# Larger row blocks in fewer places: a masked prefix sum read from HBM in blocks of 1024 rows

**Chip, cores, metric.** One core of one Trainium2 chip. The metric is the device time of one execution in microseconds (us), the median of several executions. An execution over 1.5% above the fastest of the same kernel is called slow. A verdict is "same", "faster" or "slower" against a bound of 2%, and "unclear" where the interval lies across it.

**Words.** The engines are TensorE (matrix products, PE in the profiles), VectorE (DVE), ScalarE (ACT), GpSimd (POOL) and SyncE (SP, which issues most loads). A *descriptor* is one contiguous piece of a transfer, one packet in the transfer records (of 2 to 16 KB for the rows of x); the page shows 16 transfer engines. The *granted clock* is TensorE's clock as a share of full speed: in the kernel before, eight matmuls of a block took 1.90 us where it was 0.5 (at 44.47 us), sixteen of the rests the same 1.90 us where it was 1.0 (at 72.95). The *landing records* are the trace's 16 marks per transfer, one for each engine's part; a transfer has landed with the last of them. All times in a trace count from the span's start. A timeline line reads: start, duration, engine, line, operation, what it writes <- what it reads, shapes, count, and in brackets the idle time before it and what ended it.

## The reference

```python
B, S, D = 8, 8192, 512          # x: [B, S, D] float32, w: [D, D], lengths: [B]
mask = (pos < lengths[:, None, None])
cs = np.cumsum(x * mask, axis=1)
mid_features = cs[b_idx, lengths // 2, :]
return np.matmul(mid_features[:, None, :], w).squeeze(1)
```

Row `lengths // 2` of the prefix sum is the sum of the first n = min(lengths // 2 + 1, lengths) rows of each batch. So the kernel reads n rows per batch (14,680 of 65,536 in this draw), adds them with matmuls, and multiplies the eight sums by `w`. With 2 KB per row it is a kernel that reads.

## The kernel before

Rows come in three kinds. **Blocks** have 512 rows and go through seven places in turn; the first blocks of batches 0 and 1 are loaded *blind*, before the lengths are known. What is left of a batch is its **rest**, up to 511 rows, loaded in parts of 256, 128, 64 and at most 64 rows into one of two rest places, which are zeroed once. One more block of the last batch (**`last`**) is loaded at the very end and folded in after the sum. The recorded texts call the blocks *items*, counted from 0, and rest 0 to rest 7 are those of batches 0 to 7; the loop takes one place after another in rounds, and each of the first four rounds adds two rests.

```python
    G = 4
    BLK = P * G                 # 512 rows, 8 KB per partition and descriptor
    BLIND = 2
    NS = 7
    PARTS = [(256, 0, 2, 4), (128, 1, 4, 4), (64, 3, 4, 2)]
    # ... (cut)
    def take(eng, s, n):                       # wait for n and take it back
        eng.wait_ge(s, n).then_inc(s, -n)

        def load(k):                           # SyncE: refill place k when it is free
            take(sp, s_free[k], 1)
            sp.dma_start(
                out=xt[:, k], in_=xf[ds(sp.snap(at[k]), BLK)].rearrange("(p g) d -> p g d", g=G)
            ).then_inc(s_full[k], 16)
    # ... (cut: ScalarE loads the rests, VectorE works out weights and addresses)
        with pe.Fori(0, pe.snap(rounds, min_val=B // 2, max_val=ROUNDS)):   # TensorE
            def add_item(k):
                keep_busy()                    # two bf16 matmuls on nothing, for the clock
                take(pe, s_full[k], 16)
                for j in range(G):
                    mm = add(j, cur[:, k], xt[:, k, j])
                mm.then_inc(s_done[k], 1)      # VectorE then sets new weights and frees the place
            nested(pe, left, BLIND, add_item)
            with pe.If_cmp(rest_rounds, 1, "IS_GE"):
                for q in range(2):
                    take(pe, s_rem[q], 16 * (len(PARTS) + 1))
                    for j in range(G):
                        mm = add(j, cur_rem[:, q, j * B:(j + 1) * B], rem[:, q, j])
                    mm.then_inc(s_rdone[q], 1)
            nested(pe, left, NS, add_item, BLIND)
        tell()                                 # the signal: the sum is complete
    # ... (cut: copy, fold with last, transpose, product with w, output)
```

## Time and profile before

| | before |
|---|---|
| median of the first 3 executions | 86.8 us (86.62 to 87.42) |
| span of the profiled execution | 84.9 us |
| read from HBM | 31.23 MB, 419 GB/s between 10 and 76.5 us |
| TensorE matmul busy | 56.6 us (67% of the span) |
| VectorE, ScalarE, GpSimd busy | 18.7, 3.7, 3.0 us |

### The profile page before, as it was taken

The numbers are of one execution on the slowest core, as the hardware profiler recorded it, in microseconds if no ns is written. First come the engines' busy times: TensorE is split into PE (matmuls) and PEld (weight loads), VectorE is DVE, ScalarE is ACT, GpSimd is POOL, SyncE is SP. The second block draws the span as 40 slices with busy tenths as digits, with TensorE's granted clock in tenths as the row PEclk, the third lists the DMA queues.
The fourth block names the chain that finished last, engine by engine and source line by source line (L and its number), as shares of the span: only waits on it lengthen the run. The fifth ranks groups of instructions, "written<-read, shape, count | busy, mean of one in ns | idle before, by whom it ended". The sixth has DMA issues, their size and how long they took to land. (4 is left out here: it accounts for less than half of the span.)

```text
span 84.9 us, 1511 instructions
## 1 busy us (share of the span) xinstructions
PE 56.6 (67%) x387; PEld 10.8 (13%) x391; DVE 18.7 (22%) x94; ACT 3.7 (4%) x5; POOL 3.0 (4%) x11
## 2 busy tenths in 40 slices
PE   2602000699999999984609855998528699999730
PEld 2002000101111112111000101211101011212410
DVE  3788888600200101100000000101000000002320
ACT  3910000000000000000000000000000000000020
POOL 5061000000000000000000000000000000000000
PEclk9999999999999999999995799999997556999999
DMA  2899999999999999999999999999999999993000
GB/s 39 309 417 428 404 422 420 422 413 424 428 428 428 413 409 428 413 413 424 428 394 424 424 428 413 413 428 424 424 403 430 424 421 409 422 403 129 2 1 14
DMA packets 4839, 31.30 MB, mean 369 GB/s; under 512 B 674, under 2 KB 690, under 8 KB 1218
## 3 DMA queue, kind: packets, MB, share of 16 engines
q1 hardware_dynamic: 3906, 27.27, 77.4%
q10 hardware_dynamic: 928, 3.97, 12.0%
q8 instruction: 2, 0.03, 0.1%
q14 instruction: 3, 0.02, 0.1%
HBM read 31.23 MB, written 0.02 MB: 368 GB/s over the span
## 5 line engine op out<-in xcount | busy, mean ns | idle before, releaser
L449 PE MATMUL s_ps<-xt,cur 128*8 128x512 f32 x200 | 30.2, 679 | 10.4 <-PEq L138 10.4
L462 PE MATMUL idle_ps<-idle 128*128 128x512 bf16 x46 | 16.4, 436 | 8.9 <-DVE addr L290 8.3
L413 DVE TENSOR_TENSOR cur<-since 128x8 f32 x18 | 3.1, 173 | 34.7 <-DVEq L138 34.7
L449 PE MATMUL s_ps<-rem,cur_rem 128*8 128x512 f32 x64 | 7.6, 592 | 0.0
L462 PEld LDWEIGHTS idle_ps<-idle 128*128 128x128 bf16 x50 | 2.9, 100 | 32.5 <-issue 32.5
L449 PEld LDWEIGHTS s_ps<-xt,cur 128*8 128x8 f32 x200 | 3.3, 87 | 23.6 <-issue 23.6
L290 DVE COPY s_sb<-s_ps 128x256 f32<-128x256 f32 x2 | 0.9, 426 | 18.7 <-PE idle_ps L466 18.7
L263 ACT COPY o_sb<-o_ps 8x128 f32<-8x128 f32 x2 | 0.5, 258 | 76.8 <-PE o_ps L529 76.8
L473 PE MATMUL s_ps<-zero 1*128 1x512 f32 x2 | 2.1, 1135 | 1.5 <-DVE zero L290 1.5
L476 PE MATMUL n_ps<-n_f,ones 1*128 1x8 f32 x2 | 0.6, 368 | 3.3 <-DVE n_f L290 3.3
L449 PEld LDWEIGHTS s_ps<-rem,cur_rem 128*8 128x8 f32 x64 | 1.8, 93 | 5.5 <-issue 5.5
L422 DVE COPY cur_rem<-table 128x32 f32 x6 | 1.1, 182 | 3.8 <-DVEq L138 3.8
L215 ACT ACTIVATE rem<-rem 128x2048 uint32<-128x2048 uint32 x1 | 1.9, 1909 | 0.0
L279 POOL MEMSET rem<- 128x2048 f32 x1 | 1.8, 1804 | 2.9 <-DVE addr L290 2.9
L290 DVE CAST n_f<-n_i 1x8 f32<-1x8 int32 x1 | 1.7, 1656 | 0.0
L529 PE MATMUL o_ps<-wt,t_sb 128*8 128x128 f32 x32 | 1.1, 273 | 0.5 <-DVE t_sb L290 0.5
L215 ACT ACT_TABLE_LOAD x1 | 1.3, 1283 | 1.3 <-PEq L552 1.3
L455 PE MATMUL t_ps<-last,e_last 128*8 128x128 f32 x32 | 1.2, 273 | 0.1
L476 PEld LDWEIGHTS n_ps<-n_f,ones 1*128 1x128 f32 x2 | 0.5, 308 | 4.8 <-DVE n_f L290 4.8
L290 DVE TENSOR_TENSOR part_a<-since,step_a 1x35 f32<-1x35 f32 (+1 forms) x2 | 1.0, 518 | 0.1
L529 PEld LDWEIGHTS o_ps<-wt,t_sb 128*8 128x8 f32 x32 | 0.8, 89 | 0.7 <-issue 0.7
L290 DVE TENSOR_TENSOR since<-item,begin 1x35 f32<-1x35 int32 (+1 forms) x2 | 0.8, 401 | 0.1
(68 smaller groups left out, 14.2 us busy)
## 6 DMA issues: line engine op xcount, KB each, us to landing
xt<-in_x_dram SPq DMA_DIRECT2D x25, 1024.0 KB, 16.3
rem<-in_x_dram ACTq DMA_DIRECT2D x3, 512.0 KB, 6.9
wt<-in_w_dram ACTq DMA_DIRECT2D x1, 1024.0 KB, 7.4
last<-in_x_dram SPq DMA_DIRECT2D x2, 512.0 KB, 17.4
rem<-in_x_dram ACTq DMA_DIRECT2D x3, 256.0 KB, 6.3
rem<-in_x_dram ACTq DMA_DIRECT2D x3, 128.0 KB, 6.5
rem<-in_x_dram ACTq DMA_DIRECT2D x3, 32.0 KB, 5.8
rem<-in_x_dram ACTq DMA_DIRECT2D x1, 64.0 KB, 6.0
```

Source lines behind the costliest of these rows:

```text
L215: act.memzero(rem[:, 0]).then_inc(s_rfree[0], 1)
L263: copy = act.copy(out=o_sb[1][:, j * P:(j + 1) * P], in_=o_ps[64 + 32 * j:64 + 32 * j + B, :P])
L279: pool.memset(rem[:, 1], 0.0).then_inc(s_rfree[1], 1)
L290: do(*args, **kw).then_inc(s_dve, 1)
L413: dve.tensor_tensor(out=cur[:, k], in0=since[:, :B, here].rearrange("p b o -> p (b o)"), in1=since[:, 1:, here].rearrange("p b o -> p (b o ...
L422: dve.tensor_copy(out=cur_rem[:, q], in_=rests[:, ds(dve.snap(of, min_val=1, max_val=B // 2 - 1), 1), q].rearrange("p o w -> p (o w)"),).t ...
L449: return pe.matmul(s_ps[32 * j:32 * j + B], lhsT=weights, rhs=rows, start=False, stop=False, skip_group_check=True, tile_position=(0, 32 * j))
L455: return pe.matmul(t_ps[32 * j:32 * j + B, :P], lhsT=weights, rhs=row[:, P * j:P * (j + 1)], start=False, stop=False, skip_group_check=Tru ...
L462: pe.matmul(idle_ps[:], lhsT=idle[:, :P], rhs=idle[:], start=True, stop=True)
L473: pe.matmul(s_ps[:], lhsT=zero[:], rhs=zero[:, :1].to_broadcast((1, D)), start=True, stop=False, skip_group_check=True)
L476: pe.matmul(n_ps[:, :B], lhsT=ones[:], rhs=n_f[:], start=True, stop=True).then_inc(s_pe, 1)
L529: mm = pe.matmul(o_ps[32 * j:32 * j + B, :P], lhsT=t_sb[:, kc, :B], rhs=wt[:, kc, j * P:(j + 1) * P], start=(kc == 0), stop=(kc == KC - 1) ...
```

## The change

The intent: fewer, larger transfers. Blocks become 1024 rows (16 KB per partition), three places in place of seven. The two blind loads become half blocks that share place 0; `last` is a half block too. Rests grow to up to 1023 rows, in five parts. Both rest places are zeroed by ScalarE; four idle matmuls in place of two run ahead of each block, which is meant to keep the clock up. In each round the first rest is added behind the second block, the second rest behind the third. The core of the diff:

```diff
-    G = 4
+    G = 8
     BLK = P * G
-    BLIND = 2
-    NS = 7
+    HALF = BLK // 2
+    FROM, TO = 2, B - 1
+    NS = 3
-    PARTS = [(256, 0, 2, 4), (128, 1, 4, 4), (64, 3, 4, 2)]
+    PARTS = [(512, 0, 2, 0, 8), (256, 1, 4, 0, 8), (128, 3, 4, 0, 4), (64, 3, 4, 4, 6)]
@@ blind loads
-            out=xt[:, b], in_=xf[b * S:b * S + BLK].rearrange("(p g) d -> p g d", g=G)
-        ).then_inc(s_full[b], 16)
+            out=xt[:, 0, b * (G // 2):(b + 1) * (G // 2)],
+            in_=xf[b * S:b * S + HALF].rearrange("(p g) d -> p g d", g=G // 2),
+        ).then_inc([s_blind, s_full[0]][b], 16)
@@ ScalarE
-        act.memzero(rem[:, 0]).then_inc(s_rfree[0], 1)
-        act.wait_ge(s_len1, 16)
+        for q in range(2):
+            act.memzero(rem[:, q]).then_inc(s_rfree[q], 1)
+        act.wait_ge(s_dve, DVE_LEFT)
@@ GpSimd
-        pool.memset(rem[:, 1], 0.0).then_inc(s_rfree[1], 1)
@@ TensorE
-            for _ in range(2):
+            for _ in range(4):
                 pe.matmul(idle_ps[:], lhsT=idle[:, :P], rhs=idle[:], start=True, stop=True)
@@ TensorE's round (VectorE's follows it)
-            nested(pe, left, BLIND, add_item)
-            (rest 0, rest 1)
-            nested(pe, left, NS, add_item, BLIND)
+            nested(pe, left, NS - 1, add_item)
+            add_rest(0)
+            nested(pe, left, NS, add_item, NS - 1)
+            add_rest(1)
```

More of the change, by code (lines that the diff above doesn't have):

```diff
@@ L46 @@
     B, S, D = x.shape
-    G = 4
+    G = 8
     BLK = P * G
-    BLIND = 2
-    NS = 7
-    ROUNDS = -(-(B * S // 2 // BLK - 1) // NS)
+    HALF = BLK // 2
+    FROM, TO = 2, B - 1
+    NS = 3
+    ROUNDS = -(-(B * S // 2 // BLK + 1) // NS)
     ITEMS = ROUNDS * NS
     KC = D // P
-    PARTS = [(256, 0, 2, 4), (128, 1, 4, 4), (64, 3, 4, 2)]
+    PARTS = [(512, 0, 2, 0, 8), (256, 1, 4, 0, 8), (128, 3, 4, 0, 4), (64, 3, 4, 4, 6)]
     WT = G * B
@@ L76 @@
     xt = sb("xt", [P, NS, G, D])
-    last = sb("last", [P, G, D])
+    last = sb("last", [P, G // 2, D])
     rem = sb("rem", [P, 2, G, D])
@@ L81 @@
     n_i = sb("n_i", [1, B], I32)
-    n_f = sb("n_f", [1, B])
+    n_f = sb("n_f", [1, 2, B])
     ones = sb("ones", [1, P])
@@ L85 @@
     idle = sb("idle", [P, D], BF16)
-    special = sb("special", [P, B])
+    special = sb("special", [1, B])
+    half1 = sb("half1", [1, B])
+    left2 = sb("left2", [1, B, 2], I32)
+    first_i = sb("first_i", [1, B], I32)
     one8 = sb("one8", [P, B])
-    cnt, blocks, has, usual, begin = [sb(n, [P, B + (n == "begin")], I32 if n in ("cnt", "blocks") else F32)
-                                      for n in ("cnt", "blocks", "has", "usual", "begin")]
-    blocks1, has1, usual1, begin1 = [sb(n + "1", [1, B + (n == "begin")], I32 if n == "blocks" else F32)
-                                     for n in ("blocks", "has", "usual", "begin")]
+    cnt, has, blocks, usual, begin = [sb(n, [P, B + (n == "begin")], I32 if n in ("cnt", "blocks") else F32)
+                                      for n in ("cnt", "has", "blocks", "usual", "begin")]
+    blocks1, usual1, begin1 = [sb(n + "1", [1, B + (n == "begin")], I32 if n == "blocks" else F32)
+                               for n in ("blocks", "usual", "begin")]
     step_c = sb("step_c", [1, B - 1])
@@ L105 @@
     meta = sb("meta", [1, 4], I32)
-    cur = sb("cur", [P, NS, B])
+    cur = sb("cur", [P, 2, NS, B])
     e_last = sb("e_last", [P, B])
@@ L132 @@
     s_last = [sem(f"last{h}") for h in range(2)]
-    s_w, s_len1, s_out = sem("w"), sem("len1"), sem("out")
+    s_w, s_len1, s_blind, s_out = sem("w"), sem("len1"), sem("blind"), sem("out")
     s_pool, s_dve, s_pe, s_act = sem("pool"), sem("dve"), sem("pe"), sem("act")
@@ L149, in less @@
         eng.reg_alu(n, n, 0, ALU.max)
-    DVE_SEL, DVE_ADDR, DVE_N, DVE_MASK, DVE_ALL = 2, 21, 23, 56, 64
+    DVE_SEL, DVE_ADDR, DVE_LEFT, DVE_N, DVE_MASK, DVE_ALL = 2, 22, 24, 26, 62, 70
     DVE_LAST = DVE_ALL + 6
@@ L159 @@
     nc.scalar.dma_start(out=wt[:], in_=w.rearrange("(p kc) d -> p kc d", kc=KC)).then_inc(s_w, 16)
-    for b in range(BLIND):
+    for b in range(FROM):
         nc.sync.dma_start(
-            out=xt[:, b], in_=xf[b * S:b * S + BLK].rearrange("(p g) d -> p g d", g=G)
-        ).then_inc(s_full[b], 16)
+            out=xt[:, 0, b * (G // 2):(b + 1) * (G // 2)],
+            in_=xf[b * S:b * S + HALF].rearrange("(p g) d -> p g d", g=G // 2),
+        ).then_inc([s_blind, s_full[0]][b], 16)
     block = nc.Block(no_gpsimd_drain=True)
@@ L185, in _ @@
         sp.wait_ge(s_dve, DVE_ADDR)
-        sp.load([left] + at[BLIND:], addr[:, BLIND - 1:NS])
-        nested(sp, left, NS, load, BLIND)
+        sp.load([left] + at[1:], addr[:, :NS])
+        nested(sp, left, NS, load, 1)
         sp.wait_ge(s_dve, DVE_ALL)
@@ L198, in _ @@
         with sp.If_cmp(facts[2], 1, "IS_GE"):
-            from_rows = xf[ds(sp.snap(facts[3]), BLK)].rearrange("(p g) d -> p g d", g=G)
+            from_rows = xf[ds(sp.snap(facts[3]), HALF)].rearrange("(p g) d -> p g d", g=G // 2)
             for h in range(2):
@@ L209, in _ @@
         alu = act.reg_alu
-        base, at, t = [act.alloc_register(f"act_{n}") for n in ("base", "at", "t")]
+        at, t = [act.alloc_register(f"act_{n}") for n in ("at", "t")]
         words = [act.alloc_register(f"act_n{i}") for i in range(4)]
         pair, top = act.alloc_register("act_pair"), 2 * B - 4
-        act.reg_mov(base, 0)
         act.reg_mov(pair, 0)
-        act.memzero(rem[:, 0]).then_inc(s_rfree[0], 1)
-        act.wait_ge(s_len1, 16)
+        for q in range(2):
+            act.memzero(rem[:, q]).then_inc(s_rfree[q], 1)
+        act.wait_ge(s_dve, DVE_LEFT)
         with act.Fori(0, B // 2):
-            act.load(words, lens1[:, ds(act.snap(pair, min_val=0, max_val=top), 4)])
+            act.load(words, left2[:].rearrange("o b n -> o (b n)")[:, ds(act.snap(pair, min_val=0, max_val=top), 4)])
             for q in range(2):
-                n = words[2 * q]
-                alu(t, n, 1, ALU.logical_shift_right)
-                alu(t, t, 1, ALU.add)
-                alu(n, t, n, ALU.min)
+                n, base = words[2 * q:2 * q + 2]
                 take(act, s_rfree[q], 1)
-                for count, start, step, g in PARTS:
+                for count, start, step, a, b in PARTS:
                     alu(t, n, count, ALU.bitwise_and)
@@ L230, in _ @@
                         act.dma_start(
-                            out=rem[start::step, q, :g],
-                            in_=rows(act, at, base, t, count).rearrange("(p g) d -> p g d", g=g),
+                            out=rem[start::step, q, a:b],
+                            in_=rows(act, at, base, t, count).rearrange("(p g) d -> p g d", g=b - a),
                         ).then_inc(s_rem[q], 16)
@@ L240, in load_last @@
                 def load_last(count):
-                    to = rem[3::4, q, 2:] if count > 32 else rem[3:4 * count:4, q, 2:3]
+                    to = rem[3::4, q, 6:] if count > 32 else rem[3:4 * count:4, q, 6:7]
                     act.dma_start(
@@ L256, in _ @@
                             act.sem_inc(s_rem[q], 16)
-                alu(base, base, S, ALU.add)
             alu(pair, pair, 4, ALU.add)
@@ L270, in _ @@
         pool.iota(item[:], pattern=[[1, ITEMS]], base=0, channel_multiplier=0)
-        pool.iota(item_a[:], pattern=[[BLK, ITEMS]], base=BLK - BLIND * BLK, channel_multiplier=0)
+        pool.iota(item_a[:], pattern=[[BLK, ITEMS]], base=HALF - BLK, channel_multiplier=0)
+        pool.iota(first_i[:], pattern=[[S, B]], base=0, channel_multiplier=0)
         pool.iota(pid[:], pattern=[[0, 1]], base=0, channel_multiplier=1)
@@ L274, in _ @@
         pool.iota(fold_i[:], pattern=[[-1, B]], base=128, channel_multiplier=1).then_inc(s_pool, 1)
-        for k in range(BLIND, NS):
+        for k in range(1, NS):
             pool.sem_inc(s_free[k], 1)
         pool.memset(idle[:], 1.0).then_inc(s_pool, 1)
-        pool.wait_ge(s_dve, DVE_ADDR)
-        pool.memset(rem[:, 1], 0.0).then_inc(s_rfree[1], 1)
     @block.vector
@@ L299, in _ @@
         step(dve.memset, special[:], 0.0)
-        step(dve.memset, special[:, :BLIND], 1.0)
-        step(dve.memset, special[:, B - 1:], 1.0)
+        step(dve.memset, special[:, :FROM], float(HALF))
+        step(dve.memset, special[:, TO:], float(HALF))
         step(dve.memset, one8[:], 1.0)
         step(dve.memset, step_c[:], float(S))
-        step(dve.memset, step_c[:, BLIND - 1:BLIND], float(S - BLK))
+        step(dve.memset, step_c[:, FROM - 1:FROM], float(S - HALF))
         dve.wait_ge(s_len1, 16)
@@ L309, in _, with begins @@
         step(dve.tensor_tensor, out=n_i[:], in0=n_i[:], in1=lens1[:, ::2], op=ALU.min)
-        def begins(cnt, blocks, has, usual, begin):
+        step(dve.scalar_tensor_tensor, out=half1[:], in0=n_i[:], scalar=float(HALF), in1=special[:],
+             op0=ALU.is_ge, op1=ALU.mult)
+        step(dve.tensor_tensor, out=left2[:, :, 0], in0=n_i[:], in1=half1[:], op=ALU.subtract)
+        def begins(cnt, blocks, usual, begin):
             parts = blocks.shape[0]
-            step(dve.tensor_scalar, out=blocks[:], in0=cnt[:], scalar1=9, scalar2=None,
+            step(dve.tensor_scalar, out=blocks[:], in0=cnt, scalar1=10, scalar2=None,
                  op0=ALU.logical_shift_right)
-            step(dve.scalar_tensor_tensor, out=has[:], in0=blocks[:], scalar=1.0, in1=special[:parts],
-                 op0=ALU.is_ge, op1=ALU.mult)
-            step(dve.tensor_tensor, out=usual[:], in0=blocks[:], in1=has[:], op=ALU.subtract)
+            step(dve.tensor_copy, out=usual[:], in_=blocks[:])
             step(dve.tensor_tensor_scan, out=begin[:, 1:], data0=one8[:parts], data1=usual[:],
-                 initial=float(BLIND), op0=ALU.mult, op1=ALU.add)
+                 initial=1.0, op0=ALU.mult, op1=ALU.add)
         def sinces(begin, a, b):
@@ L333, in addresses @@
             step(dve.tensor_tensor, out=addr[:, a:b], in0=item_a[:, a:b], in1=sum_a[:, a:b], op=ALU.add)
-        begins(n_i, blocks1, has1, usual1, begin1)
-        step(dve.tensor_copy, out=addr[:, BLIND - 1:BLIND], in_=begin1[:, B:])
+        begins(left2[:, :, 0], blocks1, usual1, begin1)
+        step(dve.tensor_copy, out=addr[:, :1], in_=begin1[:, B:])
         step(dve.scalar_tensor_tensor, out=step_a[:], in0=usual1[:, :B - 1], scalar=float(-BLK), in1=step_c[:],
@@ L339, in _ @@
         dve.wait_ge(s_pool, 1)
-        sinces(begin1, BLIND, NS)
-        addresses(BLIND, NS)
+        sinces(begin1, 1, NS)
+        addresses(1, NS)
         assert done == DVE_ADDR, done
+        step(dve.tensor_copy, out=left2[:, :, 1], in_=first_i[:])
+        step(dve.tensor_tensor, out=left2[:, :FROM, 1], in0=left2[:, :FROM, 1], in1=half1[:, :FROM], op=ALU.add)
+        assert done == DVE_LEFT, done
+        step(dve.tensor_copy, out=n_f[:, 0], in_=left2[:, :, 0])
+        step(dve.tensor_copy, out=n_f[:, 1], in_=half1[:])
+        assert done == DVE_N, done
         step(dve.memset, since[:, :1], 1.0)
-        step(dve.tensor_copy, out=n_f[:], in_=n_i[:])
-        assert done == DVE_N, done
-        step(dve.memset, bits[:], 256)
+        step(dve.memset, bits[:], 512)
         step(dve.memset, thr[:], 0)
@@ L356, in _ @@
         step(dve.tensor_scalar, out=m4[:], in0=m4[:], scalar1=3, scalar2=None, op0=ALU.is_equal)
-        step(dve.tensor_tensor, out=bits[:, 2:], in0=bits[:, 2:], in1=shape(m4[:], P, 2),
+        step(dve.tensor_scalar, out=sh[:], in0=m4[:], scalar1=6, scalar2=None,
+             op0=ALU.logical_shift_left)
+        step(dve.tensor_tensor, out=bits[:, 4:], in0=bits[:, 4:], in1=shape(sh[:], P, 4),
+             op=ALU.subtract)
+        step(dve.tensor_tensor, out=bits[:, 6:], in0=bits[:, 6:], in1=shape(m4[:], P, 2),
              op=ALU.subtract)
@@ L360, in _ @@
              op0=ALU.logical_shift_right)
-        step(dve.tensor_tensor, out=thr[:, 2:], in0=thr_i[:], in1=shape(m4[:], P, 2), op=ALU.mult)
+        step(dve.tensor_tensor, out=thr[:, 6:], in0=thr_i[:], in1=shape(m4[:], P, 2), op=ALU.mult)
         step(dve.memset, since[:, B:], 0.0)
@@ L364, in _ @@
         step(dve.tensor_copy, out=cnt[:], in_=n_ps[:, :B])
-        begins(cnt, blocks, has, usual, begin)
+        step(dve.tensor_scalar, out=has[:], in0=n_ps[:, B:2 * B], scalar1=1.0, scalar2=None, op0=ALU.is_ge)
+        begins(cnt[:], blocks, usual, begin)
         sinces(begin, 0, ITEMS)
-        step(dve.tensor_tensor, out=cur[:].rearrange("p k b -> p b k"), in0=since[:, :B, :NS],
-             in1=since[:, 1:, :NS], op=ALU.subtract)
-        step(dve.memset, cur[:, :BLIND], 0.0)
-        step(dve.tensor_copy, out=cur[:, :BLIND].rearrange("p k b -> p (k b)")[:, ::B + 1], in_=has[:, :BLIND])
+        step(dve.tensor_tensor, out=cur[:].rearrange("p h k b -> p h b k"),
+             in0=shape(since[:, :B, :NS].unsqueeze(1), P, 2, B, NS),
+             in1=shape(since[:, 1:, :NS].unsqueeze(1), P, 2, B, NS), op=ALU.subtract)
+        step(dve.memset, cur[:, :, 0], 0.0)
+        step(dve.tensor_copy, out=cur[:].rearrange("p h k b -> p (h k b)")[:, :NS * B + FROM:NS * B + 1],
+             in_=has[:, :FROM])
         step(dve.memset, table[:], 0.0)
@@ L386, in _ @@
         step(dve.tensor_scalar, out=meta[:, 1:2], in0=round_f[:], scalar1=float(B // 2), scalar2=None, op0=ALU.max)
-        step(dve.tensor_copy, out=meta[:, 2:3], in_=has1[:, B - 1:])
-        step(dve.tensor_scalar, out=meta[:, 3:], in0=blocks1[:, B - 1:], scalar1=BLK,
-             scalar2=(B - 1) * S - BLK, op0=ALU.mult, op1=ALU.add)
+        step(dve.tensor_copy, out=meta[:, 2:3], in_=half1[:, B - 1:])
+        step(dve.tensor_tensor, out=meta[:, 3:], in0=left2[:, B - 1, :1], in1=left2[:, B - 1, 1:], op=ALU.add)
         assert done == DVE_MASK, done
@@ L413, in weights, with rest_weights @@
                 dve.tensor_tensor(
-                    out=cur[:, k], in0=since[:, :B, here].rearrange("p b o -> p (b o)"),
-                    in1=since[:, 1:, here].rearrange("p b o -> p (b o)"), op=ALU.subtract,
+                    out=cur[:, :, k],
+                    in0=shape(since[:, :B, here].rearrange("p b o -> p o b"), P, 2, B),
+                    in1=shape(since[:, 1:, here].rearrange("p b o -> p o b"), P, 2, B), op=ALU.subtract,
                 ).then_inc(s_free[k], 1)
-            nested(dve, left, BLIND, weights)
-            with dve.If_cmp(rest_rounds, 1, "IS_GE"):
-                for q in range(2):
+            def rest_weights(q):
+                with dve.If_cmp(rest_rounds, 1, "IS_GE"):
                     take(dve, s_rdone[q], 1)
@@ L425, in _ @@
                     ).then_inc(s_rfree[q], 1)
-            nested(dve, left, NS, weights, BLIND)
+            nested(dve, left, NS - 1, weights)
+            rest_weights(0)
+            nested(dve, left, NS, weights, NS - 1)
+            rest_weights(1)
             less(dve, rest_rounds, 1)
@@ L475, in _ @@
         pe.wait_ge(s_dve, DVE_N)
-        pe.matmul(n_ps[:, :B], lhsT=ones[:], rhs=n_f[:], start=True, stop=True).then_inc(s_pe, 1)
+        pe.matmul(n_ps[:, :2 * B], lhsT=ones[:], rhs=n_f[:].rearrange("o n b -> o (n b)"), start=True, stop=True).then_inc(s_pe, 1)
         pe.wait_ge(s_pool, 2)
@@ L482, in _ @@
         pe.reg_mov(rest_rounds, B // 2)
+        pe.wait_ge(s_blind, 16)
         with pe.Fori(0, pe.snap(rounds, min_val=B // 2, max_val=ROUNDS)):
@@ L486, in add_item, with add_rest @@
                 take(pe, s_full[k], 16)
-                for j in range(G):
-                    mm = add(j, cur[:, k], xt[:, k, j])
+                for g in range(G):
+                    mm = add(g % 4, cur[:, g // 4, k], xt[:, k, g])
                 mm.then_inc(s_done[k], 1)
-            nested(pe, left, BLIND, add_item)
-            with pe.If_cmp(rest_rounds, 1, "IS_GE"):
-                for q in range(2):
+            def add_rest(q):
+                with pe.If_cmp(rest_rounds, 1, "IS_GE"):
                     take(pe, s_rem[q], 16 * (len(PARTS) + 1))
-                    for j in range(G):
-                        mm = add(j, cur_rem[:, q, j * B:(j + 1) * B], rem[:, q, j])
+                    for g in range(G):
+                        mm = add(g % 4, cur_rem[:, q, g * B:(g + 1) * B], rem[:, q, g])
                     mm.then_inc(s_rdone[q], 1)
-            nested(pe, left, NS, add_item, BLIND)
+            nested(pe, left, NS - 1, add_item)
+            add_rest(0)
+            nested(pe, left, NS, add_item, NS - 1)
+            add_rest(1)
             less(pe, left, NS)
@@ L517, in _ @@
         with pe.If_cmp(has_last, 1, "IS_GE"):
-            mm = add_last(1)
-            mm.then_inc(s_pe, 1)
+            add_last(1).then_inc(s_pe, 1)
         with pe.Else():
```

## The prediction

> **What bounds the kernel now.** I read the page's slices first, then the times from issue to landing, then the chain and the timeline at the end, and last the prologue. The slices (40 of 2.12 us):
>
> ```profile
> PE   2602000699999999984609855998528699999730
> PEclk9999999999999999999995799999997556999999
> DMA  2899999999999999999999999999999999993000
> GB/s 39 309 417 428 404 422 420 422 413 424 428 428 428 413 409 428 413 413 424 428 394 424 424 428 413 413 428 424 424 403 430 424 421 409 422 403 129 2 1 14
> ```
>
> From slice 3 to slice 36 (4 to 76 us) the 16 transfer engines never pause. 31.23 MB are read; over 10 to 76.5 us a windows view gives 419 GB/s at DMA share 1.01. TensorE has gaps in that time, so the stream of rows is the bound. What sets the end is the last landing plus what TensorE still has to do after it:
>
> ```profile
> L181 SPq DMA_DIRECT2D xt<-in_x_dram x1: 333/333/333, 59.5 to 59.5; - x1
> DMA to landing us min/median/max: 17.2/17.2/17.2
> ...
> L201 SPq DMA_DIRECT2D last<-in_x_dram x2: 333/338/342, 60.9 to 61.4; - x2
> DMA to landing us min/median/max: 17.0/17.4/17.7
> ```
>
> The last 1 MB block (item 24) is issued at 59.5 and lands at 59.5 + 17.2 = 76.7 us; the second half of `last` lands at 61.4 + 17.7 = 79.1. The chain of waits names only TensorE from 66.8 us on:
>
> ```profile
> 74.85 0.54 PE idle_ps L462 x2
> 75.39 0.97 PE s_ps L449 x8
> 76.37 0.16 issue
> 76.52 0.38 PE idle_ps L462
> 76.90 0.98 PE s_ps L449 x8
> 77.88 0.08 PE idle_ps L466
> ```
>
> but its last block starts at 76.9, 0.2 us after that landing: TensorE had only just caught up. So the end is: landing of item 24 at 76.7, 1.2 us to the end of TensorE's adding (77.9), then a fixed tail of 84.9 - 77.9 = 7.0 us (two copies, fold, transpose, product, output). The two rests of the fourth pair were added before items 23 and 24:
>
> ```profile
> 72.95 1.90 PE L449 MATMUL s_ps<-rem,cur_rem 128*8 128x512 f32 x16
> ```
>
> 16 matmuls (8 groups of rows) take 1.90 us at full clock, and they were hidden under the stream.
>
> [...] The transfer records of the trace agree in kind: 84 ns for 2 KB, 159 for 4 KB, 309 for 8 KB (lower quartiles), a straight line with 9 ns fixed and 150 ns per 4 KB. At 8 KB the fixed part is 9/309 = 2.9%, so there is little left to win. [...] a stretch of 3.4 us with 1.39 us of matmul is followed by half clock, one with 2.20 is not.
>
> ```profile
> 37.50:40.90 3.40, 2.20 (x18) 0.26 (x10) 0.17 (x1) 0.00 (x0) 0.00 (x0) 1.00 1.01 422
> 61.40:64.80 3.40, 1.39 (x14) 0.26 (x10) 0.00 (x0) 0.00 (x0) 0.00 (x0) 1.00 1.04 423
> 64.80:68.20 3.40, 2.76 (x14) 0.28 (x10) 0.00 (x0) 0.00 (x0) 0.00 (x0) 0.50 1.01 420
> ```
>
> (third number: TensorE's busy time; third from the end: its clock.) [...]
>
> ```profile
> 4.97 1.80 POOL L279 MEMSET rem<- 128x2048 f32 x1 [2.88 <-DVE addr L290]
> 5.13 1.66 DVE L290 CAST n_f<-n_i 1x8 f32<-1x8 int32 x1
> ```
>
> Eight numbers take 1.66 us because the fill runs beside them; they end together at 6.8.
>
> **The change, part by part.** From the lengths of the draw, 14,736 rows are read by either kernel (rests are rounded up), so the bytes stay 31.23 MB. Before: 25 blocks of 512 rows and 1,424 rows of rests. After: 3 half blocks (two blind, one `last`), 10 blocks of 1024 and 2,960 rows of rests (64, 144, 256, 16, 912, 704, 800, 64).
>
> *Descriptors.* Carrying the line on, 16 KB should take 609 ns in place of 2 x 309 = 618 (estimate). Ten blocks are 8 x 10 = 80 such descriptors per engine: 80 x 9 = 0.72 us. The rests' parts of 512 and 256 rows give about 0.15 more. Gain **0.9 us** of the stream.
>
> *Prologue.* Moving the second fill from GpSimd to ScalarE frees the cast (-1.5 us); six more steps of VectorE at about 0.19 us (+1.1), `table` twice as wide (+0.3), `since` half as wide (-0.2). Reckoned step by step, the weights are ready at about 13.7 us against 14.0, and TensorE starts near 15.4 against 15.7. ScalarE's two fills of 4096 elements take 2 x 3.8 us (1.91 for 2048 before), so rests are issued from about 11.8 and not 6.1; they are needed only near 24 us. Nothing here is on the path.
>
> *Places.* Before, seven places give 7 MB ahead; now place 0 holds the blind halves, and 4 MB follow. The stream has work until about 10.1 (blind blocks and w: the first landing records of the second blind block) + 2 x 4.9 (blocks) + 1.0 (rests 0, 1) = 20.9 us; in the records one engine runs about 2.2 us behind the others, so 23 for it. TensorE frees place 0 after four idle matmuls at half clock (1.9 us, from 15.4), then eight groups, mostly at half clock: about 20.9. With the issue (0.3) and about 1 us to the first bytes (w: issued 0.89, first bytes 1.92), new rows flow from 22.1. So 15 engines pause for about 1 us, but the late one, which decides each landing, hardly does: **0 to 1 us**, 0.4 taken. Afterwards a block takes 4.9 us to load, TensorE needs 1.1 (idle matmuls) + 2.0 for it, and two further blocks are queued, so I see no second drought.
>
> *The end.* Eleven items in rounds of three make the last round items 9 and 10, **then** rest 6, **then** rest 7: the code now puts rest 0 of a round behind its second item and rest 1 behind the third, and nothing follows. `last` is queued behind item 10 and lands 2.4 us after it, so it no longer decides. Item 10 lands at 76.7 - 0.9 + 0.4 = 76.2. After it: item 10, 16 matmuls, 1.9 to 2.1; rest 6, 1.9; rest 7, 1.9; 0.2 to the signal: 6.0 us, where the old kernel had 1.2. TensorE ends at 82.2 and not 77.9: +4.3. As `last` has landed by 78.6, the 0.2 us wait for it inside the old tail goes: **+4.1**.
>
> *The clock.* Item 9 lands well before item 10, since 4.9 us of block and rest 6's transfer (800 rows, 3.8 us, sharing the engines) lie between. TensorE does its 2 us and 1.1 of idle matmuls, then waits 2 to 4 us. Such gaps halved the clock before. While it is half, 3.4 us of time do 1.7 of work. I take a chance of 0.6 that one or two windows of the last 6 us are slow, at about 2.4 us each time: **+1.4**.
>
> Sum: 86.8 + 4.1 + 1.4 = 92.3 us; a little off for a milder clock: **92.0**.
>
> **The rivals.** *A, the intended gain:* larger descriptors and fewer of them shorten the stream and the end follows it. For it: the stream fills 4 to 76 us. Against: 9 ns per descriptor is all there is, and the end is landing plus TensorE's remainder, which grows. If the rests were hidden after all, 86.8 - 0.9 + 1.0 (a longer last block) = about 87. *B, too few places:* the stream runs dry at 21 us and again when TensorE is at half clock. For it: 6 MB of places, a refill of 2 MB only after eight groups. Against: once running, 4.9 us of load exceed TensorE's 3.1. By itself +0.5 to +3 us, 87 to 90, and it would show as a hole in the slices. *C, the serial end* (mine): +4.1 at full clock, 91; *with half clock all through the end* the 5.8 us of matmuls become up to 9.5, 94.5.
>
> **Range and chances.** The lower edge is C at full clock with no drought and some slack in my matmul times: 89.5. The upper edge is C with two slow windows or a drought of 1 us: 95.0. Faster by 2% (under 85.1) would need A with twice the gain and a hidden end: 0.02. Within 2% (to 88.5) needs most of the rests' 3.8 us to be hidden: 0.09. Slower: 0.89.
>
> **What would show each step.** Descriptors: records of 16,384 bytes of about 609 ns, and 425 GB/s in the middle in place of 419. Prologue: the cast of `n_f` at about 0.15 us, the first idle matmul near 15.4. Places: the slice at 20 to 22 us below the others. The end: DMA share falls at 76 to 78 us while TensorE goes on to 82 or later, and the chain ends in 32 matmuls on `rem` just ahead of the signal; `t_ps` waits for no DMA. The clock: halves among the last five slices before the tail. I am wrong if the adding ends within 3 us of the last landing of `xt`, if the middle rate moves by over 3%, or if the stream shows holes after 25 us.

## The result, and the profile after

The changed kernel takes 90.89 us in the median (90.08 to 91.87, 4 executions) against 86.71 (86.55 to 87.42). The ratio is 1.043 with a 95% interval of 1.031 to 1.056. Ratios here are the mean time of one kernel's fast executions over that of the other's of the same rounds, so not quite the ratio of the medians. It is slower. The profiled execution (90.37 us) has a span of 88.6 us.

The slices of the changed kernel, 40 of 2.2 us:

```profile
PE   3620000999999991988939104992807995599740
PEclk9999999999999999999999996599997599999998
DMA  1899999996799999999999999999999999920000
GB/s 30 322 414 422 466 397 427 418 463 215 259 429 422 451 422 422 429 437 437 407 437 422 429 433 403 437 414 433 412 443 414 451 414 387 403 98 0 0 0 7
```

The stream has a hole at slices 10 and 11 (20 to 24 us) that the old one lacks. It ends at about the same time as before, yet TensorE is busy for two slices more. Next, the landings: the last block's issue and its time to landing, then that of the two halves of `last` (issued at 59.5 and 60.0).

```profile
L186 SPq DMA_DIRECT2D xt<-in_x_dram x1: 333/333/333, 58.5 to 58.5; - x1
DMA to landing us min/median/max: 17.7/17.7/17.7
...
DMA to landing us min/median/max: 18.4/18.7/19.1
```

The last block lands at 58.5 + 17.7 = 76.2 us (76.7 before), the second half of `last` at 60.0 + 19.1 = 79.1 (79.1 before). The chain of waits, in order of time (start, duration, what), from its beginning:

```profile
76.32 0.04 issue
76.37 5.34 PE s_ps L465 x48
81.70 0.07 PE idle_ps L482
81.78 0.02 issue
```

48 matmuls follow the last landing: 16 of the block, 32 of two rests. They take 5.3 us, and the signal comes at 81.7 where the old kernel had 77.9. The tail behind it is 88.6 - 81.8 = 6.8 us, 7.0 before. So from the last block's landing to the signal it is 5.5 us where it was 1.2. These 4.3 us are more than the whole loss of about 3.6 us of span, since the block lands 0.5 us sooner and the tail is 0.2 us shorter.

This end belongs to this draw of lengths. Eleven items make four rounds, as many as there are pairs of rests; by the code, with more items the rests would still be added in the first four rounds and blocks would follow them. No run here has another draw.

### The profile page after: what moved, and what is told of

Read it like the earlier page. It is cut to its first block, busy times and chain, and to the rows that moved or that the text cites.

```text
span 88.6 us, 1478 instructions
## 1 busy us (share of the span) xinstructions
PE 55.7 (63%) x425; PEld 14.3 (16%) x425; DVE 16.0 (18%) x90; ACT 8.9 (10%) x6; POOL 1.3 (1%) x11
## 5 line engine op out<-in xcount | busy, mean ns | idle before, releaser
L465 PE MATMUL s_ps<-xt,cur 128*8 128x512 f32 x176 | 23.5, 657 | 13.3 <-PEq L142 13.3
L478 PE MATMUL idle_ps<-idle 128*128 128x512 bf16 x44 | 12.6, 413 | 8.9 <-DVE e_last L289 8.9
L465 PE MATMUL s_ps<-rem,cur_rem 128*8 128x512 f32 x128 | 16.3, 635 | 2.7 <-PEq L142 2.7
L465 PEld LDWEIGHTS s_ps<-xt,cur 128*8 128x8 f32 x176 | 4.1, 93 | 27.1 <-issue 27.1
L425 DVE TENSOR_TENSOR cur<-since 128x16 f32 x8 | 1.5, 187 | 34.5 <-DVEq L142 34.5
L220 ACT ACTIVATE rem<-rem 128x4096 uint32<-128x4096 uint32 x2 | 7.1, 3608 | 0.0
L465 PEld LDWEIGHTS s_ps<-rem,cur_rem 128*8 128x8 f32 x128 | 3.7, 93 | 13.9 <-issue 13.9
L434 DVE COPY cur_rem<-table 128x64 f32 x6 | 1.2, 195 | 17.7 <-DVEq L142 17.7
L471 PE MATMUL t_ps<-s_sb,fold 128*8 128x128 f32 x8 | 0.8, 275 | 0.2
L471 PEld LDWEIGHTS t_ps<-last,e_last 128*8 128x8 f32 x32 | 0.8, 89 | 0.3 <-issue 0.3
## 6 DMA issues: line engine op xcount, KB each, us to landing
rem<-in_x_dram ACTq DMA_DIRECT2D x3, 512.0 KB, 12.2
rem<-in_x_dram ACTq DMA_DIRECT2D x3, 256.0 KB, 12.9
```

What stands on the lines that cost most here:

```text
L220: act.memzero(rem[:, q]).then_inc(s_rfree[q], 1)
L425: dve.tensor_tensor(out=cur[:, :, k], in0=shape(since[:, :B, here].rearrange("p b o -> p o b"), P, 2, B), in1=shape(since[:, 1:, here].rea ...
L434: dve.tensor_copy(out=cur_rem[:, q], in_=rests[:, ds(dve.snap(of, min_val=1, max_val=B // 2 - 1), 1), q].rearrange("p o w -> p (o w)"),).t ...
L465: return pe.matmul(s_ps[32 * j:32 * j + B], lhsT=weights, rhs=rows, start=False, stop=False, skip_group_check=True, tile_position=(0, 32 * j))
L471: return pe.matmul(t_ps[32 * j:32 * j + B, :P], lhsT=weights, rhs=row[:, P * j:P * (j + 1)], start=False, stop=False, skip_group_check=Tru ...
L478: pe.matmul(idle_ps[:], lhsT=idle[:, :P], rhs=idle[:], start=True, stop=True)
```

## The experiments

Each kernel ran beside the kernel before on one chip. Where a profile fell into a slow execution this is said, and only the order of things is read from it.

### Leave out the last two rests' matmuls (wrong result)

```diff
                     take(pe, s_rem[q], 16 * (len(PARTS) + 1))
-                    for g in range(G):
-                        mm = add(...)
-                    mm.then_inc(s_rdone[q], 1)
+                    with pe.If_cmp(rest_rounds, 2, "IS_GE"):
+                        for g in range(G):
+                            mm = add(...)
+                        mm.then_inc(s_rdone[q], 1)
```

> Edit: in the last round TensorE takes the two rests' landings but leaves out their 32 matmuls; loads, places and waits are as in the changed kernel. The result is wrong on purpose. Serial end (mine): the signal comes 3.6 us sooner at full clock (item 10 lands at 76.4, 7, and the wait for rest 7's landing at 78.2 comes in its place, so the signal at 78.5), and the time falls from 90.4 to about 87.2, ratio 1.005 to 1.015. Drought or slower landing as the main cause: the time stays over 89.

Ratio 1.016 (1.008 to 1.025; by the bound of 2% unclear), against 1.043 of the changed kernel: 2.7% of 86.6 = 2.3 us came back. The profile, timeline:

```profile
76.17 1.90 PE L465 MATMUL s_ps<-xt,cur 128*8 128x512 f32 x16 [1.67 <-PEq L142]
79.43 0.16 PE L482 MATMUL idle_ps<-idle 128*1 128x1 bf16 x1 [1.36 <-PEq L142]
```

Loads and places are as they were; the last block starts at 76.2, 0.2 us sooner than in the changed kernel. Without the 32 matmuls the signal comes 2.1 us sooner (81.7 to 79.6). It is less than the 3.6 us of their length, because TensorE now sits idle for 1.36 us where they were. Of these, 0.6 us are the last rest's late landing (78.7 in the landing records): rest 7 is issued at 72.6 only, since its place is freed by rest 5. The other 0.7 us are the branches that end the loop, which the trace has on TensorE's sequencer from 78.7 to 79.4; in the changed kernel they run from 79.0 to 79.4 under matmuls. These 1.4 us are nearly all that this run still lacks to the kernel before (span 86.4 against 84.9). So the work behind the last landing is most of the loss, and the late landing of the last rest sits right behind it. The ratio came out just above what I expected (1.005 to 1.015), and the signal later (78.5 expected).

### Move one of the two rests forward

```diff
-            nested(pe, left, NS - 1, add_item)
+            nested(pe, left, 1, add_item)
             add_rest(0)
-            nested(pe, left, NS, add_item, NS - 1)
+            nested(pe, left, NS, add_item, 1)
             add_rest(1)
```

(The same on VectorE.)

> Edit: only the round's first rest is moved behind its first block; rest 7 still follows item 10. Serial end: half of the dose of the run before, one rest of 16 matmuls (1.8 us) remains behind item 10: signal near 80.2, time 88.7 to 89.3, about 1.025 of before. Drought: 90 to 91, as the changed kernel.

Ratio 1.022 (1.014 to 1.031; unclear by the bound of 2%; fast 88.22 and 88.57), with a correct result. Half the dose gave 2.1% back against the first measurement of the changed kernel, about as expected (ratio 1.025). The profile is of a slow execution; it shows the order meant, with 16 matmuls of a rest behind the last block and not 32:

```profile
77.26 1.90 PE L465 MATMUL s_ps<-xt,cur 128*8 128x512 f32 x16 [0.16 <-PEq L142]
79.02 1.90 PE L465 MATMUL s_ps<-rem,cur_rem 128*8 128x512 f32 x16
```

### Move both rests forward

```diff
-            nested(pe, left, NS - 1, add_item)
+            nested(pe, left, 1, add_item)
             add_rest(0)
-            nested(pe, left, NS, add_item, NS - 1)
             add_rest(1)
+            nested(pe, left, NS, add_item, 1)
```

> Edit: in each round both rests are added behind the round's first block, so in the last round the order is item 9, rest 6, rest 7, item 10. Serial end (mine): item 10 lands near 76.4 us as in the changed kernel, TensorE adds only its 16 matmuls (1.9 us) after that and signals at 78.5 in place of 81.8; time 87.0 to 87.6, about 1.01 of before. Too few places / drought (rival B): the order of the end does not matter, the time stays at 90 to 91. Larger descriptors alone would do (rival A): under 86.0.

Expected 87.0 to 87.6; measured 89.45 in the only fast execution and 91.25 to 93.88 in the slow ones, so no interval. My expectation failed. The timeline (slow execution) shows what came in the wait's place:

```profile
65.30 3.60 PE L465 MATMUL s_ps<-rem,cur_rem 128*8 128x512 f32 x16 [8.24 <-PEq L142]
```

TensorE waits 8.24 us in the third round for rest 5 (704 rows), while blocks lie ready behind it (item 7 since 57.5 in the landing records). Rest 5's last part was issued at 45.9, and TensorE could start on the rest at 65.3 only, 19.4 us later; blocks were loaded in the same time. An order that asks for the long rests early stalls everything: item 10 takes item 7's place, so it is issued only after the stall (73.2) and lands at 80.7.

### All rests in the first two rounds, with four rest places

On top of the kernel of the next experiment:

```diff
-    rem = sb("rem", [P, 2, G, D])
+    rem = sb("rem", [P, 4, G, D])
-            (blocks and the two rests in turn, as in the changed kernel)
+            nested(pe, left, NS, add_item)
+            for q in range(4):
+                add_rest(q)                  # rest_rounds = B // 4
```

> Edit, on top of the kernel with a place of its own for the blind halves: four places for rests, four rests added at the end of each of the first two rounds, so all eight are done before the last four blocks and nothing but 16 matmuls follows the last block. Serial end (mine): last block lands near 75.8, signal 77.9 at full clock (79.5 at half), second half of last near 78.3; time 86.2 to 86.8 at full clock, 87.5 to 88.5 at half; ratio 0.995 to 1.02. If large blocks or few places cost in themselves (rival B): 89 or more in spite of it. Risk: TensorE waits for rests 4 to 7 while all three places are full, as in the first experiment; then a hole in the stream near 55 to 65 us and over 89.

This was to be a version that beats both. Ratio 1.136 (1.132 to 1.140): the risk named ahead came true, though later than named. Transfers over the slices, and TensorE's waits for rests 5 and 6:

```profile
DMA  2999999999999999999999999999300057983000
...
60.60 3.60 PE L466 MATMUL s_ps<-rem,cur_rem 128*8 128x512 f32 x16 [6.74 <-PEq L144]
70.05 5.09 PE L466 MATMUL s_ps<-rem,cur_rem 128*8 128x512 f32 x32 [5.85 <-PEq L144]
```

While TensorE waits for the rests and then adds them (to 75.1), all three places stay full. Once the last of these loads has landed (70.7), nothing is left to load until a place is free again (next block issued at 78.7): the stream stands still for three to four slices of 2.4 us. Where rests are added is bounded on both sides: too late is serial, too early stalls the places.

### A place of its own for the blind halves

```diff
+    blind = sb("blind_rows", [P, G, D])
-            out=xt[:, 0, b * (G // 2):(b + 1) * (G // 2)],
+            out=blind[:, b * (G // 2):(b + 1) * (G // 2)],
-        for k in range(1, NS):
+        for k in range(NS):
             pool.sem_inc(s_free[k], 1)
+        pe.wait_ge(s_blind, 32)              # ahead of the rounds
+        for g in range(G):
+            add(g % 4, cur_b[:, g // 4], blind[:, g])
```

(Block numbers and addresses shift by one; four idle matmuls ahead of the blind rows are cut here.)

> Edit: the two blind half blocks get a place of their own, so all three places can be loaded before TensorE has started; the order at the end is the same (last block, rest 6, rest 7). Drought (rival B): the hole at 21 to 23 us vanishes; if it is the main cause the time goes back to 87. Serial end (mine): the hole vanishes as well, but the last block lands only some 0.5 us sooner (the late engine never paused), so 89.8 to 90.2, ratio 1.035 to 1.042.

One fast execution only (89.25; the slow ones 90.76 to 91.72), so it ran again in five rounds:

> The kernel with a place of its own for the blind halves again, since only one of its executions was of the fast state (89.25). If the hole in the stream were the main cause, the fast executions would lie near 87, ratio under 1.01. By the serial end they lie at 89 to 90.5, ratio 1.03 to 1.045, with the signal of TensorE near 81 to 82 although the hole is gone.

Ratio 1.035 (1.029 to 1.041; fast 89.22, 89.80, 90.09). Windows of the changed kernel, then of this one, 20 to 23 us (the last number is GB/s, the one before it the share of the transfer engines):

```profile
20.00:23.00 3.00, 3.00 (x28) 0.86 (x28) 0.19 (x1) 0.00 (x0) 0.00 (x0) 1.00 0.64 197
```
```profile
20.00:23.00 3.00, 3.00 (x24) 0.66 (x20) 0.00 (x0) 0.00 (x0) 0.00 (x0) 1.00 1.01 431
```

The hole is gone, and the ratio falls by about 1% only (from 1.043 in the first measurement of the changed kernel, 1.048 in its repeat). Its end:

```profile
71.19 3.21 PE L467 MATMUL s_ps<-rem,cur_rem 128*8 128x512 f32 x16 [2.71 <-PEq L144]
74.33 1.37 PE L480 MATMUL idle_ps<-idle 128*128 128x512 bf16 x4
75.64 1.90 PE L467 MATMUL s_ps<-xt,cur 128*8 128x512 f32 x16
77.36 3.70 PE L467 MATMUL s_ps<-rem,cur_rem 128*8 128x512 f32 x32
```

The last block had landed by 73.5 (landing records), but TensorE came to it at 75.6, held by rest 5's late landing (71.1) and its matmuls, and two rests still follow: signal at 81.0 in place of 81.7. Taking away the hole of too few places (rival B) gave 0.7 us at the signal, so it is not the main cause of this loss. At the landings the hole is worth a little more: the second half of `last` lands at 78.0 and not 79.1, of which about 0.3 us are rest 7's 64 rows, now behind it (estimate: 131 KB at 424 GB/s). What it would cost with no rests at the end, no run shows. In one point my expectation was off: I had the last block landing 0.5 us sooner and it was 2.7, as the rests' transfers fell behind it.

### Smaller descriptors again

Each block in two or four transfers, 8 or 4 KB per descriptor:

```diff
-            sp.dma_start(out=xt[:, k], in_=...).then_inc(s_full[k], 16)
+            for h in range(n):               # n = 2 or 4; TensorE takes 16 * n
+                sp.dma_start(out=xt[:, k, part], in_=rows_k[:, part]).then_inc(s_full[k], 16)
```

> Edit: each block of 1024 rows is loaded by two transfers of 8 KB per descriptor, as before the change; all else as changed. By the records (611 ns for 16 KB, 309 for 8 KB) the stream gets 80 x 7 = 0.6 us longer: second half of last lands at 79.8 in place of 79.2, time 91.0, ratio 1.05. If large descriptors were worth more (rival A): over 92.

> Edit: each block loaded by four transfers of 4 KB per descriptor: a dose that ought to be visible. By the records (159 ns for 4 KB) 80 x (4 x 159 - 611) = 2.0 us longer stream: last lands at 81.2, time 92.4, ratio about 1.066.

Ratios 1.084 (1.075 to 1.093) and 1.108 (1.101 to 1.115): both slower than expected. The transfer records give 611 ns for 16 KB (lower quartile), 309 for 8 KB, 159 for 4 KB, as in the working. In the 8 KB profile the last block lands at 76.4 and the second half of `last` at 79.1 (landing records), at most 0.2 us later than in the changed kernel and not the 0.6 expected. The middle of the stream does run slower, 422 GB/s against 427 between 24 and 75 us (1.2% of 51 us, 0.6 us). But the hole is shallower with half transfers, 270 GB/s against 217 between 20 and 24 us, which at 427 GB/s gives back about 0.5 us (estimate from these rates). What made the difference was TensorE: it had waited twice as long for that block (4.25 us against 2.06), and its matmuls then ran at half pace for about 3.4 us (timeline: the weight loads for each four of them come 0.85 us apart from 77.7 to 80.3, and 0.43 us apart from 80.8 on; 0.85 is also what the changed kernel shows at 55.2 to 57.0, where its granted clock is 0.50):

```profile
76.53 3.15 PE L467 MATMUL s_ps<-xt,cur 128*8 128x512 f32 x16 [4.25 <-PEq L142]
79.42 4.14 PE L467 MATMUL s_ps<-rem,cur_rem 128*8 128x512 f32 x32
```

The 48 matmuls take 7.0 us and not 5.3: 1.7 of the 2.1 us between the two profiled executions. What set the waits I tested no further; I have one pair of landings, in which a rest came sooner beside blocks of smaller descriptors. The last part of rest 5 (64 rows, behind the rest's larger parts), issued at 47.3 in the changed kernel and 47.1 here, took this long to land (changed, then 8 KB):

```profile
DMA to landing us min/median/max: 19.5/19.5/19.5
```
```profile
DMA to landing us min/median/max: 12.2/12.2/12.2
```

So 16 KB descriptors are worth about 0.6 us in the middle of the stream and at most 0.2 us at its end here; most of the difference in this pair (1.7 of 2.1 us) is the clock. For 4 KB the profile is of a slow execution, and the excess over my 2.0 us is not taken apart; it stays open.

### More or no idle matmuls

`range(8)` and `range(0)` in place of `range(4)`:

> Edit: eight idle matmuls ahead of each block in place of four, order of the changed kernel. Clock: the gap of 2 us ahead of item 10 is filled with 1 us more of matmul, so the clock is full at the end in nearly every execution and the spread of the times (90.1 to 91.9) falls to 90.2 to 90.7; but the first block is added 1.9 us later (four more at half clock), so the hole in the stream at 21 to 23 us grows to some 3 us and the last landing moves by up to 1.5 us: 91 to 92 if the hole sets the landing, 90.3 if it does not. Serial end alone: no change, 90.4.

> Edit: no idle matmuls ahead of the blocks, order of the changed kernel. Clock: TensorE is idle some 3 us ahead of item 10, the clock is half there, the 48 matmuls behind the last landing take up to 9 us in place of 5.4: 91.5 to 94.5. Drought: the first block is added about 1.9 us sooner, so the hole at 21 to 23 us almost closes and the last landing comes about 0.5 us sooner: 89.8 if the clock does not matter.

Eight: ratio 1.066 (1.057 to 1.076). The expected 91 to 92 was just passed (fast 91.91 to 92.46). The profile shows why, and it is not the landing, which moved by 0.5 us only: the idle matmuls came in TensorE's way in the last round.

```profile
74.68 1.90 PE L465 MATMUL s_ps<-xt,cur 128*8 128x512 f32 x16
76.51 1.90 PE L478 MATMUL idle_ps<-idle 128*128 128x512 bf16 x8
78.34 1.90 PE L465 MATMUL s_ps<-xt,cur 128*8 128x512 f32 x16
```

The last block had landed at 76.7 (landing records) and starts 1.6 us later, behind eight matmuls on nothing. None: ratio 1.034 (1.026 to 1.043), not worse than four (1.043 and 1.048 in other rounds), although the granted clock falls to 0.84 to 0.90 (fast executions; 0.915 to 0.962 with four). I had expected 91.5 to 94.5 by the clock and 89.8 by the hole alone; the fast mean is 89.5. Its profile is of a slow execution, so how much the sooner start gives and the lower clock takes is not separated; together the idle matmuls do not pay here.

### One part alone: ScalarE's fill in the kernel before

```diff
-        act.memzero(rem[:, 0]).then_inc(s_rfree[0], 1)
+        for q in range(2):
+            act.memzero(rem[:, q]).then_inc(s_rfree[q], 1)
-        pool.wait_ge(s_dve, DVE_ADDR)
-        pool.memset(rem[:, 1], 0.0).then_inc(s_rfree[1], 1)
```

> The kernel before with one part of the change alone: the second fill of the rest places moves from GpSimd to ScalarE. By my prediction the cast of n_f falls from 1.66 to 0.16 us and TensorE starts about 1.5 us sooner, but nothing there is on the path: the last landings stay at 76.7 and 79.1 and the time at 86.6, ratio 0.995 to 1.005. If the start of TensorE counted for the end, 85.1, ratio 0.983.

Ratio 0.999 (0.993 to 1.004), on VectorE and TensorE:

```profile
5.14 0.16 DVE L289 CAST n_f<-n_i 1x8 f32<-1x8 int32 x1
14.20 1.02 PE L461 MATMUL idle_ps<-idle 128*128 128x512 bf16 x2 [8.25 <-DVE addr L289]
```

TensorE starts 1.5 us sooner (15.70 before) and the time stays: this part is not on the path.

### The changed kernel again

> The changed kernel again, in the same rounds, for the clock: 90.1 to 91.9, ratio 1.04 to 1.06; executions with a lower granted clock are the longer ones, and where the clock is half behind the last block's landing, the signal comes 1.5 to 3 us later than the 5.3 us after it of the first profile.

Ratio 1.048 (1.042 to 1.053); fast executions 90.43, 90.58, 90.64 and 91.70, slow ones up to 95.64. The result repeats. The spread goes less by the clock than I thought: 90.43 has a granted clock of 0.915 and 90.64 one of 0.96.

## Why the prediction was right

It said 92.0 us (89.5 to 95.0) and slower; measured were 90.9, and 91.8 in the repeat. By its steps:

- **Descriptors.** 609 ns were foreseen for 16 KB; 611 were measured, and 424 GB/s between 23 and 75 us where the old kernel has 419. The last block landed 0.5 us sooner as foreseen, but `last` lands at 79.1 as before: the hole took what the descriptors gave (without the hole it was 78.0).
- **Prologue.** TensorE was foreseen at 15.4 and started at 15.34; that the moved fill, which gave most of it, is off the path, the single part alone shows (0.999). One detail was wrong: ScalarE issues the first rest at 8.0 and not 11.8, since the second fill still runs (to 9.8) while it does.
- **Places.** Place 0 was foreseen free at 20.9 (VectorE's write: 20.6). I gave the hole 0 to 1 us, 0.4 taken. Removing it gave 0.7 us of signal, inside the range and above the value, and 0.8 to 1.1 us at the landing of `last`. The half pace foreseen for the start shows as well: four idle matmuls took 1.88 us at 15.34 and 1.04 at 20.21 (the trace has no clock record before 19.68). As foreseen, the late engine (in the kernel before, its mark for the second blind block comes at 12.9 and the other fifteen by 10.8) caught up with the others in the hole: the sixteen parts of item 2 landed over 2.3 us (21.1 to 23.4), those of item 3 over 0.8 us (28.1 to 28.8).
- **The end.** Foreseen: last block at 76.2, 6.0 us to the signal, +4.1 in the time. Measured: 76.2, 5.5 us, +3.6 in the span. The working added 1.9 us for each group of 16 matmuls, but in a row the groups overlap: the 32 of the rests took 3.62 us and all 48 took 5.34. Leaving the 32 matmuls out and moving 16 of them both bring back what this step says in kind. The first also shows that 1.5 us of the 3.6 are not won by that alone, as rest 7 lands late and the loop's last branches come into the open. Both were missing from the working.
- **The clock.** +1.4 was a mean over chances. With the 0.3 taken off again for a milder clock, 1.1 us of the 92.0 are the clock's. In the profiled execution the end ran at full clock (granted 1.00 from 70.9 us to past the signal), and its time is 1.6 us below the prediction: these 1.1 and the 0.5 of the end. In the 8 KB variant the end ran at half pace for about 3.4 us and cost 1.7.

One line of the working is incomplete: the 25 blocks and 1,424 rows given for the kernel before are 14,224 rows; the 512 rows of `last` make it 14,736.

So the mechanism held: the serial end is the loss. The terms that were off are the clock's (+1.1, none in the profiled execution), the end's (0.5 too much) and the hole's (0.4 taken, 0.7 to 1.1 measured). The predicted value is 1.1 us above the first median. That it is only 0.2 us above the median of the repeat is luck: half of those executions are slow, and the fast ones have a median of 90.6. None of the variants of the changed kernel beats the kernel before; the best correct one with an interval keeps one rest behind the last block (1.022).

## What to carry to other kernels

When a kernel is bound by a stream, as here, its time is the last landing plus all work that can only start then (76.2 us, then 5.5 to the signal and 6.8 behind it); count that work in the last round of the loop, with the real number of items, before counting what larger transfers save. Work with its own small set of buffers must be placed neither last (serial: 4.3 us more behind the landing here) nor so early that the main places fill up behind its wait (one of 8.24 us in one run, 6.74 and 5.85 in another). By the records here, descriptors of 8 KB leave 3% to win at most (9 of 309 ns), so the number of places and the order of the work decided.

## What else the traces show

- Transfer records, lower quartiles: 84, 159, 309 and 611 ns for 2, 4, 8 and 16 KB. Two of one size together take 9, 9 and 7 ns more than one of twice the size.
- In one pair of runs, halving the blocks' descriptors from 16 to 8 KB went with a rest part beside them landing 12.2 us after its issue and not 19.5.
- From 21 to 80 us the granted clock changes between 1.0 and 0.5 at 44.34, 47.75, 64.82 and 71.64 us in the kernel before and at 53.81, 57.22, 67.46 and 70.88 in the changed one; within each trace these lie whole multiples of 3.41 us apart (to 0.02 us). In the kernel before, the stretch from 61.40 to 64.82 held 1.41 us of matmul and was followed by half clock. In the changed kernel the stretch below, one such step after the change at 70.88, holds less, 1.35 us, and was followed by full clock. So no threshold in matmul time comes out of these runs.

```profile
74.29:77.70 3.41, 1.35 (x17) 0.42 (x20) 0.00 (x0) 0.00 (x0) 0.00 (x0) 1.00 0.99 396
```

- The sixteen engines' parts of one landing lie apart by 2.2 us for the old kernel's last block (74.5 to 76.7 in the landing records), 0.7 in the changed kernel after its hole (75.5 to 76.2), 4.6 in a slow execution of it (74.0 to 78.7).
